# First layer of the block compression on two scaled 16-bit halves, in an NSA + forgetting-attention layer

## The chip, the cores and the metric

The kernel runs on one core of a Trainium2 chip. The metric is device time in microseconds (us) of one execution, the median of several runs. The core has five engines that run beside each other, each in its own program order: TensorE (PE; loading of its weights is shown apart as PEld), VectorE (DVE), ScalarE (ACT), GpSimd (POOL) and SyncE (SP), which here issues nearly all DMAs. Products land in PSUM, the rest lives in SBUF.

## The reference

One inference step of a decoder layer over 1024 prompt tokens and 8 x 8 sample tokens (512 cached tokens each), model width 1024, all in single precision. One projection gives the inputs of two head groups: native sparse attention with three branches (compressed blocks, selected blocks, window) and forgetting attention. The part that the change touches is the compression of the first branch's keys and values:

```python
def compress(x, pe, w1, w2):                      # CMP_LEN 32, CMP_STRIDE 16, hidden 128
    n_cmp = (L - CMP_LEN) // CMP_STRIDE + 1
    idx = np.arange(n_cmp)[:, None] * CMP_STRIDE + np.arange(CMP_LEN)[None, :]
    blocks = x[:, idx] + pe[None, None, :, None, :]
    h = jax.nn.silu(jnp.einsum('bnlgd,ldh->bngh', blocks, w1))
    return jnp.einsum('bngh,hd->bngd', h, w2)
...
kcmp = rms_norm(compress(kc, pe_k, w1k, w2k), gk_cmp)
vcmp = compress(vc, pe_v, w1v, w2v)
```

It is done once for the prompt and once for each of the 8 sample sequences over their cached pages; k and v have weights of their own.

## The kernel before

**Stages.** The first third projects the tokens: `w_in` is cut into 15 chunks of 256 to 288 columns, and for each chunk nine token tiles (eight of the prompt, one of the samples) are multiplied (`project`, L245 and L238). Tokens and projection weights stand as two half-precision halves, high and low, and each product is made of three (high by high, high by low, low by high). The chunks 0 to 10 go first; the rest is strewn into the forgetting attention of the prompt, followed by the sample attention strewn into the sparse attention, and the output projection.

**Compression.** It is a list of background functions, called at the fourth tile of a chunk: `cmp_weights` and `cmp_prompt_tokens` in chunk 1, `cmp_cached(0..3)` (two sequences each) in chunks 2 to 5, `sample_compressed` in chunk 6. `cmp_pairs` (L455) loads pairs of tokens (`cpair`, four buffers), transposes them on TensorE into the PSUM tile `ctr`, of which there is one buffer (L466), and copies them from there to `cx` (prompt) or `cy` (cache) on ScalarE (L468). `cmp_acc` (L474) multiplies: for each of k and v 16 products of 128 rows into the PSUM tile `sa`, of which there is one buffer too. In single precision, with 133 columns for the prompt (its blocks and the position embedding) and 128 for a cached group. `cmp_hidden` adds the bias and applies SiLU, and a second, small product (L508, L537) follows.

**Weights of the chunks.** `load_w` loads a chunk's weights in four parts into `wst` (four buffers), squares them on ScalarE with a running sum (`vsq`, L201), adds the sums up with a product by all-ones weights (L204), takes a power on GpSimd (L207), and splits the scaled weights into halves `wsp` (L215 to L220).

**What sets the order.** The functions above are written in program order, but the compiler's scheduler, with a timeline of its own, decides the order of each engine's queue; it moves background work between the products of a chunk. Tiles with the same tag share buffers, and a buffer is written again only when its last readers are done.

Of the kernel before, what the change touches and what calls it, by code (L numbers as in the profile page):

```python
# [11 lines left out]
F32 = mybir.dt.float32  # L12
F32R = mybir.dt.float32r
F16 = mybir.dt.float16
# [79 lines left out]
def layer_kernel(ctx, tc, a, o):  # L94
# [329 lines left out]
    cbias = C.tile([128, 2, 2], F32, name="cbias")  # L424
    cw = []

    def cmp_weights():
        cw.append(C.tile([128, 2, 16, 128], F32, name="cw", tag="vb16"))
        for kv in range(2):
            w1, w2 = ((a["w_cmp1_k"], a["w_cmp2_k"]), (a["w_cmp1_v"], a["w_cmp2_v"]))[kv]  # L430
            w1v = w1[0].rearrange("(s p) d h -> (p d) s h", p=2)
            for q in range(2):
                nc.sync.dma_start(cw[0][:, kv, 8 * q:8 * q + 8], w1v[:, 8 * q:8 * q + 8])
            nc.sync.dma_start(cw2[:, kv], w2[0])
        nc.vector.tensor_scalar(cw2, cw2, 0.5, None, op0=ALU.mult)

    def cmp_hidden(acc, kv, n, dst):
        t = C.tile([128, 130], F32, name="hth", bufs=1)
        u = C.tile([128, 130], F32, name="hb", bufs=1)
        nc.vector.tensor_scalar(u[:, :n], acc, cbias[:, kv, 0:1], None, op0=ALU.add)  # L440
        nc.scalar.activation(t[:, :n], acc, AF.Tanh, scale=0.5, bias=cbias[:, kv, 1:2])
        nc.vector.scalar_tensor_tensor(dst, t[:, :n], 1.0, u[:, :n], op0=ALU.add, op1=ALU.mult)
# [12 lines left out]
    def cmp_pairs(loads, dst):  # L455

        st = []
        for load in loads:
            x = C.tile([128, 4, 2, 64], F32, name="cpair", bufs=4)
            load(x)  # L460
            st.append(x)
        for kv in range(2):
            p = PS.tile([128, 2, 2, 128], F32, name="ctr", bufs=1)
            for j in range(2):
                for g in range(2):
                    nc.tensor.transpose(p[:, j, g], st[j][:, 2 * kv + g].rearrange("m p d -> m (p d)"), ident)  # L466
            for g in range(2):
                nc.scalar.activation(dst(kv, g), p[:, :, g].rearrange("p j (c r) -> p r j c", r=8), AF.Copy)  # L468

    def cmp_acc(kv, n, view):  # L470
        acc = PS.tile([128, 256], F32, name="sa", bufs=1)
        for i in range(16):
            h, r = divmod(i, 8)
            nc.tensor.matmul(acc[:, 0:n], cw[0][:, kv, i], view(h, r), start=(i == 0), stop=(i == 15))  # L474
        return acc

    def cmp_prompt_tokens():
        cx = [C.tile([128, 8, 134], F32, name=f"cx{kv}", tag=f"cy{kv}") for kv in range(2)]
        pet = C.tile([32, 128], F32, name="cpe", tag="grow")
        for kv in range(2):  # L480
            nc.gpsimd.memset(cx[kv][:, :, 64:66], 0.0)
            nc.gpsimd.memset(cx[kv][:, :, 130:132], 0.0)
            nc.sync.dma_start(pet[16 * kv:16 * kv + 16], (a["pe_cmp_k"], a["pe_cmp_v"])[kv][0].rearrange("(s p) d -> s (p d)", p=2))
        p = PS.tile([128, 2, 2, 128], F32, name="ctr", bufs=1)
        nc.tensor.transpose(p[:, 0, 0, 0:32], pet, ident[0:32, 0:32])
        for kv in range(2):
            nc.scalar.activation(cx[kv][:, :, 132:134],
                                 p[:, 0, 0, 16 * kv:16 * kv + 16].rearrange("p (h r) -> p r h", h=2), AF.Copy)

        def load(k):  # L490
            def f(x):
                for p in range(2):
                    nc.sync.dma_start(x[:, :, p], cmp_prompt[k, :, p])
            return f

        for q in range(2):
            cmp_pairs([load(2 * q), load(2 * q + 1)],
                      lambda kv, g: cx[kv][:, :, g * 66 + 32 * q:g * 66 + 32 * q + 32].rearrange("p r (j c) -> p r j c", j=2))
        for kv in range(2):
            acc = cmp_acc(kv, 133, lambda h, r: cx[kv][:, r, h:h + 133])  # L500
            nc.scalar.activation(cbias[:, kv, 0:1], acc[:, 132:133], AF.Copy)
            nc.scalar.activation(cbias[:, kv, 1:2], acc[:, 132:133], AF.Copy, scale=0.5)
# [11 lines left out]
    def cmp_cached(q):  # L514
        cy = [C.tile([128, 8, 4, 34], F32, name=f"cy{kv}", tag=f"cy{kv}") for kv in range(2)]
        for y in cy:
            nc.gpsimd.memset(y[:, :, :, 32:34], 0.0)
        for b in range(2):
            def load(k):
                def f(x):  # L520
                    for j in range(2):
                        src = cmp_pages[ds(page(2 * q + b, 2 * k + j), 1)]
                        for p in range(2):
                            nc.sync.dma_start(x[64 * j:64 * j + 64, :, p], src[:, :, p].rearrange("o m z d -> (o m) z d"))
                return f
            cmp_pairs([load(0), load(1)],
                      lambda kv, g: cy[kv][:, :, 2 * g + b, 0:32].rearrange("p r (j c) -> p r j c", j=2))
        for kv in range(2):
            acc = cmp_acc(kv, 128, lambda h, r: cy[kv][:, r, :, h:h + 32])
# [1083 lines left out]
```

## Time and profile before

| what | us |
|---|---|
| median of 3 runs | 976.82 |
| lowest and highest | 975.48, 977.11 |
| the profiled execution | 974.53 |
| its span | 972.8 |
| TensorE busy | 901.1 |
| VectorE, ScalarE, GpSimd busy | 644.9, 612.3, 397.4 |

The span goes from the first to the last instruction in the profile; the execution's own time has a little around it. Engines overlap, so their busy times don't add up to the span. A line number such as L474 is that of the kernel above. In a row of the timeline stand the start, the length of the merged piece, engine, line, operation, output and inputs, shapes and the count; idle time ahead of it and what ended it stand in brackets. A single-precision product leaves two records. Pieces of TensorE overlap, since products are pipelined, so pace is read from start to start.

### The profile page before, as it was taken

Reading aid. Unit: us, or ns where it says so; the run is one execution under the profiler, and the core shown is the slowest. Engines: PE = TensorE matmul, PEld = TensorE weight load, DVE = VectorE, ACT = ScalarE, POOL = GpSimd, SP = SyncE. Lnnn points to the kernel's source line nnn. Section 1 sums busy time; section 2 is a strip of 40 time slices with the busy share of each in tenths; the row PEclk is TensorE's granted clock in tenths of the full one; section 3 lists DMA queues with packets and bytes.
Section 4 is the critical chain, followed back from the end, with each engine's and each line's share of the span. In section 5 each row is a group of like instructions: output and inputs, shape, how many; then the busy total and the mean of one; then the engine's idle time right before and its main releaser. Section 6 shows DMA issues by size and latency. Waiting matters only on the chain.

```text
span 972.8 us, 24636 instructions
## 1 busy us (share of the span) xinstructions
PE 901.1 (93%) x9097; PEld 707.1 (73%) x9097; DVE 644.9 (66%) x1845; ACT 612.3 (63%) x1328; POOL 397.4 (41%) x571
## 2 busy tenths in 40 slices
PE   4898999889999999999998888889999979999997
PEld 3687889878888988878786556656666645776776
DVE  5764666564555426768777566887888989776552
ACT  6844643433454665797786779888897868454540
POOL 4544567754676432342425123434333157211100
PEclk9999999999999999999999899999999999999999
DMA  7563323422343332331314755555355032231241
GB/s 267 142 154 110 90 81 89 107 59 70 98 117 99 117 106 65 106 110 54 88 43 125 234 154 154 164 170 177 114 167 185 5 129 97 97 108 57 76 140 66
DMA packets 119740, 111.73 MB, mean 115 GB/s; under 512 B 37100, under 2 KB 100244, under 8 KB 119596
## 3 DMA queue, kind: packets, MB, share of 16 engines
q1 hardware_dynamic: 117732, 106.74, 36.4%
q0 software_dynamic: 1456, 2.83, 1.3%
q8 instruction: 71, 1.16, 0.5%
q10 hardware_dynamic: 432, 0.59, 0.2%
q14 instruction: 49, 0.40, 0.1%
HBM read 79.57 MB, written 27.41 MB: 110 GB/s over the span
## 4 chain that ended last, share of the span: by engine, by line
PE 64%; DVE 9%; DMA 7%; ACT 6%; issue 3%; POOL 2%; SPq 1%; DVEq 0%; ACTq 0%; POOLq 0%
PE acc L245 22%; PE ctr L1499 7%; PE sa L474 3%; PE acc L238 3%; PE smax L1054 2%; PE pv L726 2%; PE pv L724 2%; PE pv L725 2%; PE st L1098 2%; PE st L1099 2%; DMA wst<-in_w_in_dram 2%; DVE junk L744 2%; PE ctr L1547 1%; PE st L774 1%; PE st L775 1%
## 5 line engine op out<-in xcount | busy, mean ns | idle before, releaser
L245 PE MATMUL acc<-wsp,xth 128*128 128x256 f16 (+1 forms) x1920 | 334.7, 275 | 5.1 <-ACT xth L175 2.6
L245 PE MATMUL acc<-wsp,xtl 128*128 128x256 f16 (+1 forms) x960 | 264.1, 275 | 0.0
L245 PEld LDWEIGHTS <-xth 128*128 128x128 f16 x1920 | 187.3, 99 | 33.7 <-ACT xth L175 3.1
L1103 ACT ACTIVATE pf<-st,nsc 128x512 f32<-128x512 f32 x132 | 99.0, 780 | 49.6 <-PE st L1099 26.9
L245 PEld LDWEIGHTS <-xtl 128*128 128x128 f16 x960 | 94.5, 98 | 14.8 <-issue 1.4
L724 PEld LDWEIGHTS <-phi 128*128 128x128 f16 x816 | 76.9, 97 | 17.0 <-issue 5.5
L726 PEld LDWEIGHTS <-plo 128*128 128x128 f16 x816 | 76.7, 99 | 9.8 <-DVE plo L1106 2.4
L1104 ACT ACTIVATE phi<-pf 128x1024 f16<-128x1024 f32 (+1 forms) x76 | 71.7, 948 | 14.0 <-PE pv L726 8.8
L725 PEld LDWEIGHTS <-phi 128*128 128x128 f16 x816 | 76.8, 97 | 4.7 <-issue 1.5
L1106 DVE TENSOR_TENSOR plo<-pf,phi 128x1024 f16<-128x1024 f32 (+1 forms) x58 | 67.0, 1158 | 10.8 <-ACT phi L1104 10.0
L711 ACT ACTIVATE pf<-st,nsc 128x512 f32<-128x512 f32 (+1 forms) x96 | 62.5, 670 | 16.1 <-PE st L775 5.2
L264 POOL TENSOR_TENSOR nss<-nss,nhalf 128x4 f32<-128x4 f32 (+3 forms) x72 | 68.4, 950 | 4.4
L724 PE MATMUL pv<-va,phi 128*128 128x65 f16 x528 | 59.0, 193 | 4.3 <-DVE nt L1083 3.4
L716 DVE TENSOR_TENSOR plo<-pf,phi 128x512 f16<-128x512 f32 (+3 forms) x77 | 51.6, 674 | 16.0 <-ACT phi L714 15.7
L201 ACT ACTIVATE vsq<-wst 128x512 f16<-128x512 f32 (+2 forms) x72 | 40.2, 559 | 33.4 <-DMA wst<-in_w_in_dram 32.5
L725 PE MATMUL pv<-va,phi 128*128 128x64 f16 x528 | 58.9, 195 | 0.0
L726 PE MATMUL pv<-va,plo 128*128 128x65 f16 x528 | 56.4, 192 | 0.4 <-DVE plo L1106 0.2
L1106 POOL TENSOR_TENSOR plo<-pf,phi 128x1024 f16<-128x1024 f32 (+1 forms) x18 | 34.6, 1923 | 51.4 <-ACT phi L1104 40.6
L714 ACT ACTIVATE phi<-pf 128x512 f16<-128x512 f32 (+1 forms) x96 | 48.7, 524 | 10.3 <-PE pv L726 8.8
L1054 PE MATMUL smax<-kma,nqm 88*128 88x512 f16 (+3 forms) x192 | 49.1, 316 | 3.8 <-DVE nm L744 3.5
L1084 POOL TENSOR_TENSOR oa<-oa,nt 128x256 f32<-128x256 f32 x22 | 19.7, 894 | 78.8 <-DVE nt L1083 65.0
L1098 PE MATMUL st<-nqm,kma 88*128 88x512 f16 x132 | 50.2, 380 | 0.9 <-ACT pf L1103 0.7
(446 smaller groups left out, 2402.6 us busy)
## 6 DMA issues: line engine op xcount, KB each, us to landing
wst<-in_w_in_dram SPq DMA_DIRECT2D x56, 256.0 KB
sfk<-in_cache_fox_kv_dram SPq DMA_DIRECT2D x32, 256.0 KB
sfv<-in_cache_fox_kv_dram SPq DMA_DIRECT2D x32, 256.0 KB
out_dram<-kv SPq DMA_DIRECT2D x52, 128.0 KB
xin<-in_x_prompt_dram SPq DMA_DIRECT2D x8, 512.0 KB
cpair<-in_cache_nsa_cmp_kv_dram SPq DMA_DIRECT2D x64, 64.0 KB
zpark<-z SPq DMA_DIRECT2D x32, 128.0 KB
spg<-in_cache_nsa_slc_kv_dram SPq DMA_DIRECT2D x32, 128.0 KB
```

Source lines behind the costliest of these rows:

```text
L245: nc.tensor.matmul(ps[:, :n], x[:, k, t * 128:(t + 1) * 128], w[k // 2][:, i, k % 2, :n], start=(k == 0 and j == 0), stop=(k == KT - 1 and ...
L264: nc.gpsimd.tensor_tensor(ss[:n, 0, :h], ss[:n, 1, :h], nhalf[:n, :h], op=ALU.pow)
L711: nc.scalar.activation(p[:n, :cols], ps[:n, :cols], AF.Exp, bias=nsc[:n, 3:4], scale=nsc[:n, 6:7])
L724: nc.tensor.matmul(po[:, s, 0:65], hi[:, c], v[:, 0:65], start=f, stop=False, skip_group_check=True)
L725: nc.tensor.matmul(po[:, s, 0:64], hi[:, c], v[:, 65:129], start=False, stop=False, skip_group_check=True)
L726: nc.tensor.matmul(po[:, s, 0:65], lo[:, c], v[:, 0:65], start=False, stop=l, skip_group_check=True)
L1054: nc.tensor.matmul(pr[:, r], qm[0:88, (r0 + r) * 128:(r0 + r + 1) * 128], kma[0:88, 2 * k + g, j0 * 128:j1 * 128], start=r == 0, stop=not ...
L1098: nc.tensor.matmul(ps, kma[0:88, 2 * k + g, c], qm[0:88], start=True, stop=False)
L1103: nc.scalar.activation(pf[:, 512 * x:512 * x + 512], ps, AF.Exp, bias=nsc[:, 3:4], scale=nsc[:, 2:3])
L1104: nc.scalar.activation(hi[:, 0:n], pf[:, 0:n], AF.Copy)
L1106: (nc.gpsimd if turn[0] % share[mixed[0]] == 0 else nc.vector).tensor_sub(lo_[:, 0:n], pf[:, 0:n], hi[:, 0:n])
L1499: nc.tensor.matmul(ps, l[:, k], w[:, k, c], start=(k == 0 and j == 0), stop=(k == KT - 1 and j == 2))
```

## The change

The first layer's weights and tokens are held as two half-precision halves instead of in single precision. Weights (one scale each for k and v) and each group of tokens (likewise) are scaled by a power of their sum of squares, and the scales are taken out again in the bias and the activation. Each of the 16 single-precision products becomes three half-precision products.

```diff
+    def cmp_sums(sq, n):
+        p = PS.tile([128, 16], F32, name="sa", bufs=1)
+        nc.tensor.matmul(p[:, 0:2 * n], ones, sq.rearrange("p k n -> p (k n)"), start=True, stop=True)
+        s = C.tile([128, 2, 2], F32, name="cssum")
+        nc.vector.tensor_reduce(out=s[:, 0], in_=p[:, 0:2 * n].rearrange("p (k n) -> p k n", k=2), axis=AX.X, op=ALU.add)
+        nc.vector.tensor_scalar(s[:, 1], s[:, 0], 2.0 ** -30, TINY, op0=ALU.mult, op1=ALU.add)
+        return s
+
     def cmp_weights():
-        cw.append(C.tile([128, 2, 16, 128], F32, name="cw", tag="vb16"))
+        cw.append(C.tile([128, 2, 16, 2, 128], F16, name="cw", tag="vb16"))
...
-                nc.sync.dma_start(cw[0][:, kv, 8 * q:8 * q + 8], w1v[:, 8 * q:8 * q + 8])
+                r = B.tile([128, 8, 128], F32, name="xin", bufs=5)
+                nc.sync.dma_start(r, w1v[:, 8 * q:8 * q + 8])
+                junk = B.tile([128, 8, 128], F32, name="xsq")
+                nc.scalar.activation(junk, r, AF.Square, accum_out=sq[:, kv, q:q + 1])
+                raw.append(r)
...
+        s = cmp_sums(sq, 2)
+        nc.gpsimd.tensor_tensor(cws[:, :, 0], s[:, 1], nhalf[:, 0:2], op=ALU.pow)
+        for kv in range(2):
+            for q in range(2):
+                hi, lo = (cw[0][:, kv, 8 * q:8 * q + 8, z] for z in (0, 1))
+                nc.scalar.activation(hi, raw[2 * kv + q], AF.Copy, scale=cws[:, kv, 0:1])
+                nc.vector.scalar_tensor_tensor(lo, raw[2 * kv + q], cws[:, kv, 0:1], hi, op0=ALU.mult, op1=ALU.subtract)
...
+    def cmp_scales(sq, n):
+        s = cmp_sums(sq, n)
+        nc.gpsimd.tensor_tensor(cws[:, :, 1], s[:, 1], nhalf[:, 0:2], op=ALU.pow)
+        nc.vector.tensor_tensor(s[:, 0], cws[:, :, 0], cws[:, :, 1], op=ALU.mult)
+        nc.vector.reciprocal(cws[:, :, 2], s[:, 0])
+        nc.vector.tensor_scalar(cws[:, :, 3], cws[:, :, 2], 0.5, None, op0=ALU.mult)
...
-    def cmp_pairs(loads, dst):
+    def cmp_load(loads, sq):
...
+            for kv in range(2):
+                junk = C.tile([128, 2, 2, 64], F32, name="cjunk", bufs=1)
+                nc.scalar.activation(junk, x[:, 2 * kv:2 * kv + 2], AF.Square, accum_out=sq[:, kv, i:i + 1])
...
+    def cmp_halves(kv, p, hi, lo):
+        nc.scalar.activation(hi, p, AF.Copy, scale=cws[:, kv, 1:2])
+        nc.vector.scalar_tensor_tensor(lo, p, cws[:, kv, 1:2], hi, op0=ALU.mult, op1=ALU.subtract)
...
             for g in range(2):
-                nc.scalar.activation(dst(kv, g), p[:, :, g].rearrange("p j (c r) -> p r j c", r=8), AF.Copy)
+                cmp_halves(kv, p[:, g].rearrange("p j m -> p (j m)").rearrange("p (c r) -> p r c", r=8), *dst(kv, g))
...
-            nc.tensor.matmul(acc[:, 0:n], cw[0][:, kv, i], view(h, r), start=(i == 0), stop=(i == 15))
+            for j, (w, x) in enumerate(((0, 0), (0, 1), (1, 0))):
+                nc.tensor.matmul(acc[:, 0:n], cw[0][:, kv, i, w], view(x, h, r), start=(i == 0 and j == 0),
+                                 stop=(i == 15 and j == 2))
```

In `cmp_prompt_tokens` and `cmp_cached` all four pairs are now loaded and squared by `cmp_load`, `cmp_scales` follows, and then come the transposes, two pairs at a time as before. The prompt's position embedding is squared too and shares the prompt's scale.

The scheduler's order changes with it. On TensorE, around the first products of the compression (the prompt's keys), the order before reads as follows; `cx` are the prompt's tokens, `acc` the projection:

```order
L245 MATMUL acc<-wsp,xtl 128x256
L466 MATMUL ctr<-ident,cpair 128x128 x4
L474 MATMUL sa<-cx_992,cw 128x133 x16
L245 LDWEIGHTS xth
L245 MATMUL acc<-wsp,xth 128x256
```

and in the changed kernel, where L508 are the transposes and L517 the products:

```order
L517 LDWEIGHTS cw
L517 MATMUL sa<-cx_1020,cw 128x133
L245 LDWEIGHTS xth
L245 MATMUL acc<-wsp,xth 128x288
L245 LDWEIGHTS xtl
L245 MATMUL acc<-wsp,xtl 128x288
L245 LDWEIGHTS xth
L245 MATMUL acc<-wsp,xth 128x288
L245 LDWEIGHTS xth
L245 MATMUL acc<-wsp,xth 128x288
L508 MATMUL ctr<-ident,cpair 128x128 x4
L517 LDWEIGHTS cw
```

The first product now stands in the next chunk (288 columns), and the last transposes stand between the first product and the other 47.

On ScalarE, the copies out of `ctr` of the second cached group (`cy`) stand before among squares of chunk weights (L201) and of projections (L261):

```order
L261 ACTIVATE nsq<-acc 128x256
L201 ACTIVATE vsq,vst<-wst 128x2x256
L468 ACTIVATE cy_2197<-ctr 128x8x32 x2
L201 ACTIVATE vsq,vst<-wst 128x2x256
L261 ACTIVATE nsq<-acc 128x256
L201 ACTIVATE vsq,vst<-wst 128x2x256 x2
L468 ACTIVATE cy_2198<-ctr 128x8x32 x2
```

and in the changed kernel, with the copies at L499 and the squares of the next group's token pairs at L494:

```order
L499 ACTIVATE cy_2428<-ctr,cws 128x8x32
L261 ACTIVATE nsq<-acc 128x256
L494 ACTIVATE cjunk,csq_3130<-cpair 128x256 x2
L261 ACTIVATE nsq<-acc 128x256
L499 ACTIVATE cy_2427<-ctr,cws 128x8x32
L494 ACTIVATE cjunk,csq_3130<-cpair 128x256 x2
L201 ACTIVATE vsq,vst<-wst 128x2x256
L499 ACTIVATE cy_2427<-ctr,cws 128x8x32
L201 ACTIVATE vsq,vst<-wst 128x2x256
L261 ACTIVATE nsq<-acc 128x256
L201 ACTIVATE vsq,vst<-wst 128x2x256 x2
```

The two copies of a buffer, adjacent before, are apart, and squares that wait for page loads stand between them, beside those that wait for weights.

On VectorE, late in the program at the last head of the forgetting attention, the order before is (`plo` is the low half of probabilities, `l` and `obt` end a head, `sms` are statistics of a sample's softmax):

```order
L716 TENSOR_TENSOR plo<-pf,phi 128x384
L716 TENSOR_TENSOR plo<-pf,phi 128x128
L782 RECIPROCAL l<-pv 128x4
L783 TENSOR_SCALAR l<-l,vsc 128x4
L786 TENSOR_TENSOR obt<-pv,l 128x4x64
L1227 TENSOR_REDUCE sms<-ctr 128x1
L1228 TENSOR_REDUCE sms<-ctr 128x1
```

and in the changed kernel (L716 has become L771, L782 to L786 are L837 to L841, L1227 is L1282):

```order
L771 TENSOR_TENSOR plo<-pf,phi 128x384
L791 TENSOR_TENSOR nqm<-smax,block 24x512
L771 TENSOR_TENSOR plo<-pf,phi 128x128
L1282 TENSOR_REDUCE sms<-ctr 128x1
L1283 TENSOR_REDUCE sms<-ctr 128x1
L837 RECIPROCAL l<-pv 128x4
L1284 TENSOR_SCALAR sms<-sms 128x1
L838 TENSOR_SCALAR l<-l,vsc 128x4
L841 TENSOR_TENSOR obt<-pv,l 128x4x64
```

No line of that part was edited; the sample's softmax has moved ahead of the end of the head. Between about chunk 9 and this place the order is the same in both, but for single rows.

More of the change, by code (lines that the diff above doesn't have):

```diff
@@ L453, in cmp_norm, with cmp_pairs @@
                                            op0=ALU.mult, op1=ALU.mult)
-    def cmp_pairs(loads, dst):
+    def cmp_load(loads, sq):
         st = []
-        for load in loads:
+        for i, load in enumerate(loads):
             x = C.tile([128, 4, 2, 64], F32, name="cpair", bufs=4)
             load(x)
+            for kv in range(2):
+                junk = C.tile([128, 2, 2, 64], F32, name="cjunk", bufs=1)
+                nc.scalar.activation(junk, x[:, 2 * kv:2 * kv + 2], AF.Square, accum_out=sq[:, kv, i:i + 1])
             st.append(x)
+        return st
+    def cmp_halves(kv, p, hi, lo):
+        nc.scalar.activation(hi, p, AF.Copy, scale=cws[:, kv, 1:2])
+        nc.vector.scalar_tensor_tensor(lo, p, cws[:, kv, 1:2], hi, op0=ALU.mult, op1=ALU.subtract)
+    def cmp_pairs(st, dst):
         for kv in range(2):
@@ L494, in load @@
             return f
+        st = cmp_load([load(k) for k in range(4)], sq)
+        cmp_scales(sq, 5)
+        p = PS.tile([128, 2, 2, 128], F32, name="ctr", bufs=1)
+        nc.tensor.transpose(p[:, 0, 0, 0:32], pet, ident[0:32, 0:32])
+        for kv in range(2):
+            cmp_halves(kv, p[:, 0, 0, 16 * kv:16 * kv + 16].rearrange("p (h r) -> p r h", h=2),
+                       *(cx[kv][:, z, :, 132:134] for z in range(2)))
         for q in range(2):
-            cmp_pairs([load(2 * q), load(2 * q + 1)],
-                      lambda kv, g: cx[kv][:, :, g * 66 + 32 * q:g * 66 + 32 * q + 32].rearrange("p r (j c) -> p r j c", j=2))
+            cmp_pairs(st[2 * q:2 * q + 2],
+                      lambda kv, g: [cx[kv][:, z, :, g * 66 + 32 * q:g * 66 + 32 * q + 32]
+                                     for z in range(2)])
         for kv in range(2):
-            acc = cmp_acc(kv, 133, lambda h, r: cx[kv][:, r, h:h + 133])
-            nc.scalar.activation(cbias[:, kv, 0:1], acc[:, 132:133], AF.Copy)
-            nc.scalar.activation(cbias[:, kv, 1:2], acc[:, 132:133], AF.Copy, scale=0.5)
+            acc = cmp_acc(kv, 133, lambda x, h, r: cx[kv][:, x, r, h:h + 133])
+            nc.scalar.activation(cbias[:, kv, 0:1], acc[:, 132:133], AF.Copy, scale=cws[:, kv, 2:3])
+            nc.scalar.activation(cbias[:, kv, 1:2], acc[:, 132:133], AF.Copy, scale=cws[:, kv, 3:4])
             hs = C.tile([128, 130], F32, name="chs", tag="qsp", bufs=1)
@@ L514, in cmp_cached, with load, f @@
     def cmp_cached(q):
-        cy = [C.tile([128, 8, 4, 34], F32, name=f"cy{kv}", tag=f"cy{kv}") for kv in range(2)]
+        cy = [C.tile([128, 2, 8, 4, 34], F16, name=f"cy{kv}", tag=f"cy{kv}") for kv in range(2)]
+        sq = C.tile([128, 2, 4], F32, name="csq4")
         for y in cy:
-            nc.gpsimd.memset(y[:, :, :, 32:34], 0.0)
-        for b in range(2):
[L519 to L527, printed above, removed]
+            nc.gpsimd.memset(y[:, :, :, :, 32:34], 0.0)
+        def load(b, k):
+            def f(x):
+                for j in range(2):
+                    src = cmp_pages[ds(page(2 * q + b, 2 * k + j), 1)]
+                    for p in range(2):
+                        nc.sync.dma_start(x[64 * j:64 * j + 64, :, p], src[:, :, p].rearrange("o m z d -> (o m) z d"))
+            return f
+        st = cmp_load([load(b, k) for b in range(2) for k in range(2)], sq)
+        cmp_scales(sq, 4)
+        for b in range(2):
+            cmp_pairs(st[2 * b:2 * b + 2],
+                      lambda kv, g: [cy[kv][:, z, :, 2 * g + b, 0:32] for z in range(2)])
         for kv in range(2):
-            acc = cmp_acc(kv, 128, lambda h, r: cy[kv][:, r, :, h:h + 32])
+            acc = cmp_acc(kv, 128, lambda x, h, r: cy[kv][:, x, r, :, h:h + 32])
             hs = C.tile([128, 130], F32, name="chs", tag="qsp", bufs=1)
```

23 lines of the change are left out of this document (13 added, 10 removed).

## The prediction

> **What bounds the kernel now.** I read the engine totals and the chain that ended last first, then the busy time by stretch, then the waits of TensorE (PE) in the stretch that the change touches, then the rows of the instructions themselves.
>
> ```profile
> PE 901.1 (93%) x9097; PEld 707.1 (73%) x9097; DVE 644.9 (66%) x1845; ACT 612.3 (63%) x1328; POOL 397.4 (41%) x571
> ...
> PE 64%; DVE 9%; DMA 7%; ACT 6%; issue 3%; POOL 2%; SPq 1%; DVEq 0%; ACTq 0%; POOLq 0%
> PE acc L245 22%; PE ctr L1499 7%; PE sa L474 3%; PE acc L238 3%; PE smax L1054 2%; PE pv L726 2%; PE pv L724 2%; PE pv L725 2%; PE st L1098 2%; PE st L1099 2%; DMA wst<-in_w_in_dram 2%; DVE junk L744 2%; PE ctr L1547 1%; PE st L774 1%; PE st L775 1%
> ```
>
> TensorE is busy for 93% of the span and holds 64% of the chain. The products that the change rewrites (L474) are 3% of the chain, some 29 us, so they are worth having on the path. The next table has the stretch, its length, then busy us and instructions of PE, weight load, DVE, ACT and POOL, then the clock and the DMA.
>
> ```profile
> 50.00:80.00 30.00, 27.35 (x248) 24.33 (x246) 18.15 (x79) 14.58 (x43) 12.80 (x24) 1.00 0.67 177
> 80.00:250.00 170.00, 162.20 (x1459) 144.14 (x1458) 99.29 (x353) 72.73 (x214) 102.04 (x176) 1.00 0.31 81
> ```
>
> The compression runs from about 50 to 250 us, strewn between the projection products of chunks 1 to 5. In the main stretch PE is busy 162 of 170 us at full granted clock, while ACT, DVE and POOL have 97, 71 and 68 us free. The waits of PE from 45 to 300 us are these three (total, times, longest):
>
> ```profile
> PE ctr L466 <- ACT cy L468: 6.0, 4, 2.6
> PE ctr L466 <- ACT cx L468: 2.6, 1, 2.6
> PE ctr L537 <- DVE lw L607: 1.8, 1, 1.8
> ```
>
> PE waits 8.6 us for the one PSUM buffer `ctr` that the transposes of token pairs share, and hardly for anything else. So a microsecond taken from PE here is nearly a microsecond of the kernel, unless the new work on ACT and DVE makes those waits longer. One of them, in rows:
>
> ```profile
> 112.00 0.63 ACT L201 ACTIVATE vsq<-wst 128x512 f16<-128x512 f32 x1 [1.41 <-DMA wst<-in_w_in_dram]
> ...
> 113.90 0.66 ACT L468 ACTIVATE cy<-ctr 128x256 f32<-128x256 f32 x2
> ...
> 114.62 0.55 PE L466 MATMUL ctr<-ident,cpair 128*128 128x128 f32 x3 [0.75 <-ACT cy L468]
> ```
>
> ACT works in order; a square of the next chunk's weights waits for its DMA, the copy that empties `ctr` stands behind it, and PE waits for the copy. The copies themselves take 0.66 us.
>
> **The change part by part: the products.** One set of products (one of k or v, one group of blocks) is 16 single-precision products before and 48 half-precision ones after. There are ten sets: two of 133 columns for the prompt and eight of 128 for the cache.
>
> ```profile
> 118.73 3.74 PE L474 MATMUL sa<-cy,cw 128*128 128x128 f32 x32
> 122.31 0.28 PE L245 MATMUL acc<-wsp,xth 128*128 128x288 f16 x1
> ...
> 77.07 3.81 PE L474 MATMUL sa<-cx,cw 128*128 128x133 f32 x32
> 80.72 0.38 PE L245 MATMUL acc<-wsp,xth 128*128 128x256 f16 x2
> ...
> 703.77 0.20 PE L726 MATMUL pv<-va,plo 128*128 128x65 f16 x1
> ...
> 704.14 0.19 PE L726 MATMUL pv<-va,plo 128*128 128x65 f16 x1
> 704.17 0.61 PE L1027 MATMUL smax<-ident,nqs 128*128 128x128 f16 x8
> 704.61 0.38 PE L1098 MATMUL st<-nqm,kma 88*128 88x512 f16 x1
> ```
>
> From its own start to the start of what follows, a set takes 122.31 - 118.73 = 3.58 us at 128 columns (32 records, two for each product) and 80.72 - 77.07 = 3.65 us at 133. The nearest half-precision row is eight products of 128 columns, each with weights of its own, in 704.61 - 704.17 = 0.44 us: 55 ns each. That the weight load isn't the limit there shows in the products of 65 columns above them, which also load 128x128 weights each time: 12 steps in 704.14 - 703.77 = 0.37 us, 31 ns each. So 48 products take 48 x 55 ns = 2.64 us, and 2.74 us at 133 columns. The gain is 0.94 us for each of eight sets and 0.91 for each of two: 7.5 + 1.8 = **9.3 us off PE**.
>
> A rule speaks against this. The Trainium skill, "TensorE: Matmul & The Clock Gate", section "Back-to-back issue gap", gives some 81 ns for each product of 128 columns in a sustained stream of weight loads and products. By it a set would take 48 x 81 = 3.89 us, more than now, and the ten sets would cost some 3 us. The trace of this kernel doesn't agree: 55 ns with a load each, 31 ns at 65 columns.
>
> **Small products.** Six sums (one of the weights, five of tokens) go through PE as a product of a few single-precision columns with all-ones weights. The kernel has that already:
>
> ```profile
> 135.74 0.27 PE L245 MATMUL acc<-wsp,xtl 128*128 128x256 f16 x1
> 135.85 0.28 PE L204 MATMUL tr<-vst,ones 128*128 128x4 f32 x2
> 136.00 0.38 PE L245 MATMUL acc<-wsp,xth 128*128 128x256 f16 x2
> ```
>
> It takes the place of 136.00 - 135.85 = 0.15 us, so six add **0.9 us**. Transposes and second-layer products stay as they are. PE in sum: -9.3 + 0.9 = -8.4 us.
>
> **ACT and DVE.** The new work, with its nearest rows:
>
> ```profile
> L201 ACT ACTIVATION_READ_ACCUMULATOR vsq<-wst 128x1 f32 x20 | 3.8, 189 | 0.0
> L261 ACT ACTIVATE nsq<-acc 128x256 f32<-128x256 f32 x27 | 10.2, 378 | 18.2 <-PE acc L245 18.2
> L468 ACT ACTIVATE cy<-ctr 128x256 f32<-128x256 f32 x32 | 10.4, 380 | 8.4 <-PE ctr L466 8.4
> L219 ACT ACTIVATE wsp<-wst,vst 128x512 f16<-128x512 f32 x10 | 7.2, 716 | 8.3 <-POOL vst L207 8.3
> L307 DVE SCALAR_TENSOR_TENSOR vb<-acc,un,vb 128x256 f16<-128x256 f32 x16 | 7.8, 485 | 21.9 <-ACT vb L306 20.7 <-PE acc L238 1.2
> L220 DVE SCALAR_TENSOR_TENSOR wsp<-wst,vst,wsp 128x512 f16<-128x512 f32 x16 | 15.0, 937 | 6.2 <-ACT wsp L219 5.9 <-DMA slp<-in_cache_fox_logf_dram 0.2
> L206 DVE TENSOR_SCALAR vst<-vst 128x1 f32<-128x1 f32 x10 | 1.5, 149 | 0.1
> ...
> L207 POOL TENSOR_TENSOR vst<-vst,nhalf 128x1 f32<-128x1 f32 x6 | 3.5, 582 | 0.4
> ```
>
> ACT squares 40 halves of token pairs with a running sum: 40 x (0.378 + 0.189) = 22.7 us. The four weight quarters of 1024 columns are squared and scaled to 16 bits; I take two 512-column rows for each pass: 4 x 2 x (2 x 0.716) = 11.5 us at most. The 40 copies out of `ctr` stay, at 0.38 us each. DVE gets 40 remainders of 256 columns out of PSUM, 40 x 0.485 = 19.4 us, four of the weights at up to 2 x 0.937, 7.5 us, and some 27 operations on two columns, 27 x 0.149 = 4.0 us. POOL gets six small powers, 6 x 0.582 = 3.5 us. In the long stretch that would put ACT at (72.7 + 34) / 170 = 63% and DVE at about (99.3 + 31) / 170 = 77%, even with all of it inside. No engine passes PE, so I cost this work at nothing; what hides it is the 162 us of projection and compression products. If that cover were gone, it is ACT's 34 us that would show.
>
> **The release of `ctr`.** Before, the buffer comes free 0.66 us after the transposes. After, it takes copy, remainder, remainder: 0.38 + 2 x 0.485 = 1.35 us, and waits in two queues. But the order of PE has moved too: between two groups of transposes of one cached set stood 26 to 36 projection products, now 41 to 60. One product is the 48th part of this:
>
> ```profile
> 136.14 5.26 PE acc L245 x48
> ```
>
> That is 110 ns, so the distance grows from 2.9-4.0 us to 4.5-6.6 us. Less the release, 2.2-3.3 us were left for queues before, 3.1-5.2 us are left now. I take the 8.6 us of waits as unchanged: nothing gained and nothing lost, with zero and about three times their size as ends.
>
> **Loads.** The same four weight DMAs now land in the token buffers `xin`, earlier. In SP's order the first stands right behind the last token tile, and two stand ahead of chunk 2's weights, which PE needs only a chunk later. All four pairs must be there before the first transpose, and ACT's squares stand in line for them. DMA bytes don't change. I cost both at nothing; a late pair stalls ACT, as under the rival below.
>
> **The later half.** The scheduler's order changes again from the last attention heads on, where nothing was edited. There PE waits for many things a little:
>
> ```profile
> 600.00:700.00 100.00, 91.05 (x1117) 62.88 (x1114) 83.95 (x268) 81.78 (x165) 39.69 (x54) 0.98 0.52 161
> 700.00:760.00 60.00, 57.02 (x778) 39.37 (x778) 47.00 (x124) 53.04 (x107) 19.08 (x26) 1.00 0.49 150
> ```
>
> PE is idle 12 of 160 us. A new order may save or add a third of that, so 4 us either way; I take zero.
>
> **Sum.** The profiled execution took 974.53 us, 1.7 us more than its span; less 8.4 us that is 966.1. The median before is 976.82, 2.3 us above the profiled one, so against the median I forecast **968.4 us**, with 964 to 974 as its own range from the later half and small shifts in the waits.
>
> **Rivals.**
>
> *The transposes wait longer (slower).* Place: `ctr`, between two groups of transposes. DVE is a second queue in the release, and these are the longest waits of each:
>
> ```profile
> DVE nx L279 <- POOL nss L264: 28.5, 27, 3.4
> ACT vsq L201 <- DMA wst<-in_w_in_dram: 21.2, 15, 4.2
> ```
>
> It decides once the queues together hold more than the 3.1 us left; 4.2 + 3.4 would. The five waits before average 1.7 us. If 15 of the 20 groups waited that long, it would be 25.8 us in place of 8.6: 976.8 - 8.4 + 17.2 = 985.6 us. Against it stands that most of those DVE waits are near 1 us (28.5 / 27). Chance 0.18.
>
> *The gain is lost elsewhere (no change).* The pace is then set by the weight loading (ACT waits 21 us for it) or the later order takes 6 to 10 us back. Time 975 to 979. Against it: PE never waits for `wsp` in that stretch. Chance 0.14.
>
> *The waits vanish (faster still).* With more products between the transposes all 8.6 us may go: 976.8 - 8.4 - 8.6 = 959.8 us. Against it: their cause, a late DMA in ACT's line, is untouched. Chance 0.12.
>
> *Weight loads show (the products aren't faster).* If a half-precision load of 98 ns were laid bare at each product:
>
> ```profile
> L245 PEld LDWEIGHTS <-xtl 128*128 128x128 f16 x960 | 94.5, 98 | 14.8 <-issue 1.4
> ```
>
> a set takes 48 x 98 = 4.70 us, ten sets cost 11.2 more than now, with the sums 12.1: 988.9 us. The 31 ns above speak against it. Chance 0.04. The Trainium skill's 81 ns, from the page named above, would give 3.1 + 0.9, some 981 us.
>
> **How the numbers follow.** Forecast 0.52, waits vanish 0.12: faster 0.64. No change 0.14. The two slower rivals 0.18 + 0.04 = 0.22. A measurement of this kernel tells about 0.2% (2 us) from no change; the bounds are 974.9 and 978.8. The range runs from 960, the waits vanishing, to 981, which takes in half of the slower rival with fewer groups waiting; about 2 in 10 is left out.
>
> **What would show it.** Right: sets of 48 products from start to next start in 2.65 us; sums at 0.15 us each; PE waits at the transposes at or below 8.6 us; the first load of cached pages for sampling and all later work some 8 us earlier. Wrong: spacing of 80 ns or more; waits of the transposes, now named after DVE's remainder, above 17 us; ACT idle before the squares for the page DMA with PE idle behind it; or the gain present at 300 us and gone at the end, which would be the later order.

## The result, and the profile after

The changed kernel took **988.95 us** (median of 4 runs, 984.73 to 995.12) against 976.9 us before: ratio 1.0127, 95% interval 1.0089 to 1.0165. It is slower by some 12 us, where 968.4 us (960 to 981) had been forecast. Run again later beside the kernel before it took 988.85 us (ratio 1.0131 [1.0111, 1.0152]). The profiled execution took 995.12 us, the longest of the four; its span is 993.2 us. Ratios and their intervals, here and below, leave out one execution of e1 (1044.66 us at a granted clock of 0.842, where all others have 0.97 or more), and they are not always the quotient of the medians beside them. Busy totals and the chain that ended last, from the page after:

```profile
PE 905.5 (91%) x9269; PEld 705.6 (71%) x9269; DVE 671.9 (68%) x1919; ACT 646.0 (65%) x1424; POOL 402.1 (40%) x577
...
PE 49%; DVE 11%; DMA 8%; POOL 7%; ACT 6%; issue 4%; SPq 1%; DVEq 0%; ACTq 0%; POOLq 0%
```

TensorE's share of the chain fell from 64% to 49%; POOL, 2% before, has 7%. ACT grew by 34 us and DVE by 27, about what the prediction had counted. So the amounts came true and the gain did not: TensorE itself is busy for 905.5 us, 4.4 more than before, and more of the chain lies on other engines.

To find where, I cut the span at two places that both kernels have: the start of the first projection product of chunk 1, and that of chunk 11. What stands ahead of the first mark varies between executions (60.0 us in one profile of the changed kernel, 57.1 in the next), so stages are counted from there. First the kernel before, then the changed one; start and end of the stretch, its length, busy us and instructions of PE, weight load, DVE, ACT, POOL, then PE's clock and the DMA:

```profile
57.90:364.40 306.50, 294.54 (x2676) 260.47 (x2674) 162.93 (x592) 145.07 (x396) 179.16 (x289) 1.00 0.35 98
364.40:972.80 608.40, 566.54 (x6134) 413.68 (x6133) 442.01 (x1143) 425.70 (x819) 191.88 (x230) 0.98 0.38 115
```

```profile
60.00:371.50 311.50, 294.74 (x2856) 256.73 (x2855) 189.89 (x666) 174.04 (x485) 185.50 (x295) 0.98 0.33 93
371.50:993.20 621.70, 572.71 (x6134) 418.34 (x6133) 442.45 (x1143) 428.34 (x819) 190.21 (x230) 0.97 0.38 113
```

Two things show. Chunks 1 to 10, where the gain was to be, take 5.0 us more. And the rest, in which no line was edited and TensorE has the same number of records, 6134, takes 13.3 us more: it is busy for 6.2 us more on them and idle for 7.1 us more.

**In the first stretch** the products did get shorter. The timeline of PE after, at the prompt's keys (start, length, engine, line):

```profile
111.05 2.95 PE L517 MATMUL sa<-cx,cw 128*128 128x133 f16 x47
113.83 0.29 PE L245 MATMUL acc<-wsp,xtl 128*128 128x288 f16 x1
```

47 products of 133 columns take 113.83 - 111.05 = 2.78 us, 59 ns each; of 128 columns they take 2.70 us (from 191.09 us on), 57 ns each. But PE waits for other things now (waits from 45 to 300 us; total, times, longest):

```profile
PE tr L204 <- ACT vsq L201: 4.1, 1, 4.1
PE sa L517 <- ACT cy L499: 3.1, 2, 2.2
PE ctr L508 <- issue: 2.5, 2, 2.3
PE ctr L543 <- DMA cpe<-in_pe_cmp_v_dram: 1.6, 1, 1.6
PE tr L170 <- DVE xtl L176: 1.6, 1, 1.6
PE ctr L508 <- DVE cy L500: 1.3, 2, 1.1
```

A wait for `issue` is one for which the profile shows no reason. The transposes, which were the place of the slower rival, wait less than before (2.5 + 1.3 us against 8.6). The longest wait stands in the projection itself. These are the rows of ACT and of PE around it:

```profile
77.01 4.27 ACT L456 ACTIVATE cw<-xin,cws 128x1024 f16<-128x1024 f32 x4 [0.97 <-POOL cws L452]
...
83.54 0.63 ACT L201 ACTIVATE vsq<-wst 128x512 f16<-128x512 f32 x1
84.07 0.19 ACT L201 ACTIVATION_READ_ACCUMULATOR vsq<-wst 128x1 f32 x1
```

```profile
79.89 0.27 PE L245 MATMUL acc<-wsp,xtl 128*128 128x256 f16 x1
84.31 0.39 PE L204 MATMUL tr<-vst,ones 128*128 128x4 f32 x2 [4.15 <-ACT vsq L201]
85.83 0.58 PE L245 MATMUL acc<-wsp,xth 128*128 128x256 f16 x2 [1.14 <-DVE va L307]
```

ACT copies the compression's weights for 4.27 us; the squares of the next chunk's weights stand behind that, their sum (L204) stands in PE's queue ahead of projection products, and PE is idle for 4.15 + 1.14 us. The squares of the compression's own token pairs stand in ACT's line too, and ahead of them it is idle for 21.2 us (count, busy us, mean ns of one, then the idle time and what ended it):

```profile
L494 ACT ACTIVATE cjunk<-cpair 128x256 f32<-128x256 f32 x40 | 16.6, 415 | 21.2 <-DMA cpair<-in_cache_nsa_cmp_kv_dram 19.0 <-DMA cpair<-out_dram 1.8
```

The granted clock halves behind the wait at L204, and once more later (windows after; the clock is the figure before the last two):

```profile
84.60:91.40 6.80, 5.67 (x28) 4.14 (x29) 4.61 (x23) 3.17 (x9) 5.67 (x13) 0.50 0.15 49
149.50:152.90 3.40, 3.40 (x34) 3.40 (x33) 3.05 (x10) 2.11 (x7) 3.03 (x6) 0.50 0.88 254
```

In these 10.2 us PE is busy for 5.67 + 3.40 = 9.07 us, so half clock cost up to 4.5 us, an estimate. Before, the same stretch ran at full clock throughout. That is the largest part of why PE's busy time did not fall although its products did.

### The profile page after: what moved, and what is told of

Its sections match the earlier page's. It is cut to its first block, busy times and chain, and to the rows that moved or that the text cites. A ratio compares the mean times of both kernels' runs of the same rounds, so it can differ in the third digit from the quotient of the medians.

```text
span 993.2 us, 25195 instructions
## 1 busy us (share of the span) xinstructions
PE 905.5 (91%) x9269; PEld 705.6 (71%) x9269; DVE 671.9 (68%) x1919; ACT 646.0 (65%) x1424; POOL 402.1 (40%) x577
## 4 chain that ended last, share of the span: by engine, by line
PE 49%; DVE 11%; DMA 8%; POOL 7%; ACT 6%; issue 4%; SPq 1%; DVEq 0%; ACTq 0%; POOLq 0%
PE acc L245 13%; PE ctr L1554 7%; POOL nss L264 2%; PE pv L781 2%; PE pv L780 2%; PE pv L779 2%; PE st L1153 2%; PE smax L1109 2%; PE st L1154 2%; DVE plo L1161 1%; DMA nq<-qpark 1%; PE acc L238 1%; PE st L829 1%; PE st L830 1%; PE ctr L1602 1%
## 5 line engine op out<-in xcount | busy, mean ns | idle before, releaser
L779 PEld LDWEIGHTS <-phi 128*128 128x128 f16 x816 | 78.0, 98 | 16.4 <-issue 3.6
L780 PEld LDWEIGHTS <-phi 128*128 128x128 f16 x816 | 77.9, 99 | 3.3 <-issue 0.5
L771 DVE TENSOR_TENSOR plo<-pf,phi 128x512 f16<-128x512 f32 (+3 forms) x77 | 51.9, 680 | 15.0 <-ACT phi L769 13.7
L1153 PE MATMUL st<-nqm,kma 88*128 88x512 f16 x132 | 50.8, 385 | 6.9 <-ACT pf L1158 6.7
L769 ACT ACTIVATE phi<-pf 128x512 f16<-128x512 f32 (+1 forms) x96 | 49.2, 528 | 10.1 <-PE pv L781 7.8
L201 ACT ACTIVATE vsq<-wst 128x512 f16<-128x512 f32 (+2 forms) x72 | 40.3, 564 | 23.7 <-DMA wst<-in_w_in_dram 23.2
L799 DVE CUSTOM_DVE_ANT_0 junk<-smax,maskw,nm 128x512 bf16<-128x512 f32 x64 | 47.7, 745 | 6.9 <-PE smax L1109 5.0
```

Of the source, the lines that this page charges most:

```text
L779: nc.tensor.matmul(po[:, s, 0:65], hi[:, c], v[:, 0:65], start=f, stop=False, skip_group_check=True)
L780: nc.tensor.matmul(po[:, s, 0:64], hi[:, c], v[:, 65:129], start=False, stop=False, skip_group_check=True)
L1153: nc.tensor.matmul(ps, kma[0:88, 2 * k + g, c], qm[0:88], start=True, stop=False)
```

## The experiments

Four questions: does the later order cost what it seems to; what in the first stretch eats the gain; is a microsecond of PE there worth one; and can the loss be avoided. Each result stands against runs of the kernel before on the same chip (974.66 us for e1 to e4, 975.64 for e5 to e8, 976.31 for e9 to e11); a difference between kernels of two of these groups is uncertain by as much as these medians differ. No kernel computes less than the reference unless it is said.

**e1: the changed kernel with the old order after chunk 11.** In all kernels here the late part has one of two orders on TensorE, apart from some 90 rows at most; small shifts of the scheduler's timeline decide which. Four idle writes, which end up at the program's start, turn it back:

```diff
     fox_operands(C2, ("km1", "qm1", "k11", "q11"))
+    nc.vector.memset(PJ.tile([128, 512], BF16, name="junk", bufs=1), 0.0)
+    nc.vector.memset(PJ.tile([128, 512], BF16, name="junk", bufs=1), 0.0)
+    nc.vector.memset(PJ.tile([128, 512], BF16, name="junk", bufs=1), 0.0)
+    nc.vector.memset(PJ.tile([128, 512], BF16, name="junk", bufs=1), 0.0)
```

> The changed kernel with four small idle VectorE memsets at the program's start. They leave its order in the first stage as it is, but the scheduler then gives the last attention heads, the sample stage and the output projection the order of the kernel before. Theory A (both matter: the first stage loses time by stalls, and the new late order loses more): the forgetting attention starts near 371 us as in the changed kernel (before: 363), and the rest runs as before, so the whole takes 980 to 984 us. Rival B (only the late order is bad): 968 to 976 us. Rival C (only the first stage and the clock are bad, the order is nothing): 987 to 991 us, as the changed kernel.

Measured 981.15 us, ratio 1.0048 [1.002, 1.0076]: theory A's range. Against the changed kernel's 988.85 that is 7.7 us for order alone. In the traces the 6134 records of PE after chunk 11 stand in e1 in the very order of the kernel before, and take 609.9 us against its 608.4.

**e2: the kernel before with the new order.** The same four writes in the kernel before give it nearly the changed kernel's late order: in the traces 61 of PE's 6134 records stand otherwise.

> The kernel before with the same four idle memsets, by which the late stages get the order of the changed kernel nearly row by row, while its first stage stays as it was. Theory A: the forgetting attention starts near 364 us, the rest is 5 to 9 us longer than before: 982 to 986 us. Rival B (only the late order is bad): 987 to 991 us. Rival C (the order is nothing): 975 to 979 us.

Measured 988.53 us, ratio 1.0119 [1.0069, 1.017]. An old kernel with old products, slowed as much as by the change. It is more than theory A expected and in theory B's range; its profile has 616.1 us after chunk 11 against 608.4 before, 7.7 us more, and chunk 11 starts 4.0 us later, 2.7 of them lost ahead of chunk 1. So the 7.7 us are the order's; why the rest is lost is not shown, and whether the idle writes take time themselves was not tried apart. That order is nothing (theory C) is refuted from both sides.

What the new order does shows in the late part of e1, cut at the transposes ahead of the output projection, and of the changed kernel's second profile (e8, below):

```profile
371.50:781.30 409.80, 380.50 (x4551) 280.73 (x4551) 307.23 (x871) 326.33 (x679) 141.78 (x190) 0.98 0.42 125
781.30:981.40 200.10, 186.94 (x1585) 134.32 (x1584) 133.92 (x273) 98.98 (x141) 50.34 (x40) 0.99 0.28 94
```

```profile
367.70:779.80 412.10, 375.50 (x4444) 278.38 (x4443) 296.49 (x849) 319.90 (x667) 139.23 (x187) 0.97 0.42 125
779.80:989.00 209.20, 195.33 (x1692) 139.24 (x1690) 146.22 (x295) 108.50 (x153) 51.03 (x43) 0.99 0.28 90
```

The orders agree up to 549 us of the changed kernel's first profile (542 in the kernel before); all of the loss lies behind that. 107 PE instructions, 8.4 us of work, moved behind the second mark, and 9.1 us more are spent there. Ahead of it PE has 5.0 us less to do, and yet that stretch takes 2.3 us longer: its idle time went from 29.3 to 36.6 us. Of the 11.4 us in all, 8.0 are idle time and 3.4 a longer busy time of PE on the same records, with 30.7 us at half clock after chunk 11 against 21.8. The waits of PE there, first e1, then e8:

```profile
PE smax L790 <- DVE mh L788: 7.0, 4, 4.9
PE ctr L1376 <- ACT sfkt L1377: 3.6, 2, 2.7
PE pv L779 <- DVE nt L1142: 3.4, 2, 2.0
...
PE st L1157 <- ACT pf L1162: 0.9, 3, 0.4
```

```profile
PE st L1153 <- ACT pf L1158: 7.1, 6, 2.5
PE smax L790 <- DVE mh L788: 6.2, 3, 4.9
PE ctr L1297 <- ACT spr L1287: 3.9, 3, 2.6
PE ctr L1352 <- ACT son L1350: 3.3, 4, 1.6
```

The scores of the sparse attention (`st`, L1153 or L1157) wait for the exponentials (`pf`) that free their PSUM: 7.1 us, 0.9 with the old order. The sample's own waits (`spr`, `son`) come on top. That less is at hand for PE just when ACT is late, since the sample's work is interleaved otherwise, is a reading of these rows; no run tries it.

**e3 and e4: constant scales.** In e3 all scales are constants (2048 for weights, 16 for tokens), so there are no squares, sums and powers; loads, halves and 48 products stay. In e4 only the weights' scale is constant. Such constants suit these inputs; they don't follow the data.

```diff
+    for i, v in enumerate((2048.0, 16.0, 1.0 / 32768, 0.5 / 32768)):
+        nc.vector.memset(cws[:, :, i], v)
...
-                nc.scalar.activation(junk, r, AF.Square, accum_out=sq[:, kv, q:q + 1])
...
-                nc.scalar.activation(junk, x[:, 2 * kv:2 * kv + 2], AF.Square, accum_out=sq[:, kv, i:i + 1])
...
-        cmp_scales(sq, 5)
...
-        cmp_scales(sq, 4)
```

> The changed kernel with constant scales: no squares of weights and tokens, no sums, no powers. Halves, remainders on VectorE and the 48 half-precision products stay; the late stages have the order of the kernel before. It leaves the computation of the scales out. Theory A, squares and scales as the cause in the first stage (ScalarE's line and the wait for all four pairs): the forgetting attention starts 6 to 9 us earlier than before, near 355 to 358 us, and the whole takes 967 to 971 us. Rival D (the remainders on VectorE and the release of ctr are the cause): it starts near 368 to 371 us and the whole takes 980 to 984 us.

> The changed kernel with a constant scale for the weights alone: their squares, their sum and the wait for it are left out, the tokens are still squared and scaled. The late order is nearly that of the kernel before. Theory A1 (the weights' work in ScalarE's line is what costs in the first stage: it held up the square of chunk 3's weights for 4.1 us and let the granted clock fall to half): the forgetting attention starts near 361 to 365 us, the whole takes 973 to 978 us. Theory A2 (the tokens' squares and their wait for page loads are what costs): it starts near 367 to 371 us, the whole takes 979 to 984 us.

e3 took 975.81 us, ratio 1.0012 [0.9985, 1.0039]; e4 984.71, ratio 1.0099 [1.007, 1.0127]. e3 missed both ranges and lies between: the squares matter, and without them the change still doesn't gain its 8 us in the total. e4 is where its second theory put it (979 to 984), if anything above: the weights' squares are nearly harmless, those of the tokens are not. The wait at L204, the longest in the changed kernel, is gone in e4, and chunk 1 to 11 still takes 309.4 us, 1.2 less than in e8; so that wait alone is not what eats the gain. Both have the old late order (609.9 and 608.8 us after chunk 11), so their difference of 9 us lies ahead of it: 7.9 us in chunks 1 to 10 (301.5 and 309.4 in the profiles) and 2.9 ahead of chunk 1. In chunks 1 to 10 e3 has gained:

```profile
61.40:362.90 301.50, 289.71 (x2844) 254.11 (x2843) 177.03 (x630) 152.12 (x399) 179.56 (x289) 0.99 0.34 96
```

301.5 us against 306.5, 5.0 of them, and 4.8 less of busy PE.

**e5: the squares alone.** The old kernel, to which the loading of four pairs at once, the 40 squares of the tokens, the sums and powers are added; their results are not used.

```diff
+            for kv in range(2):
+                junk = C.tile([128, 2, 2, 64], F32, name="cjunk", bufs=1)
+                nc.scalar.activation(junk, x[:, 2 * kv:2 * kv + 2], AF.Square, accum_out=sq[:, kv, i:i + 1])
...
+        cmp_scales(sq, 4)
```

> The old kernel with its single-precision products and plain copies, and beside them the new kernel's loading of four pairs at once, the squares of the tokens, their sums and powers, whose results nothing uses. The order from chunk 11 on is the old one but for some 30 rows. Theory A2 (the tokens' squares in ScalarE's line, with their waits for the loads, delay the projection's own work): the first stage takes 9 to 11 us more as between e3 and e4, chunk 11 starts at 372 to 375 us, the time is 982 to 986. Rival D (squares cost only because the copies need the scale that comes out of them): chunk 11 starts at 364 to 367, the time is 974 to 978.

Measured 985.4 us, ratio 1.0105 [1.0087, 1.0124]; chunk 1 to 11 took 315.5 us, 9.0 more than before:

```profile
59.40:374.90 315.50, 300.97 (x2686) 264.94 (x2684) 167.36 (x615) 160.39 (x467) 184.10 (x294) 0.98 0.34 94
```

Theory A2. Of PE's work only the sums read these squares, and none of PE's waits in that stretch is at a sum; so it isn't the longer chain to the copies that costs. This is their group on ACT in e5: count, busy us and mean ns of one, then ACT's idle time ahead of them and what ended it:

```profile
L483 ACT ACTIVATE cjunk<-cpair 128x256 f32<-128x256 f32 x40 | 16.6, 415 | 31.9 <-DMA cpair<-in_cache_nsa_cmp_kv_dram 26.4 <-DMA cpair<-out_dram 5.2
L483 ACT ACTIVATION_READ_ACCUMULATOR cjunk<-cpair 128x1 f32 x40 | 7.7, 192 | 0.0
```

24.3 us of work, as predicted (22.7), and 31.9 us in which ACT stands in front of a square whose load has not landed, up to 4.1 us at a time, with everything behind it.

**e9: the same squares without the wait for loads.** To tell standing still from working, the 40 squares of e5 read the copies that come out of the transposes instead of the loaded pairs: same size, same number, same number of sums, which now stand behind the transposes. The loading of four pairs at once stays. Against e5:

```diff
-                nc.scalar.activation(junk, x[:, 2 * kv:2 * kv + 2], AF.Square, accum_out=sq[:, kv, i:i + 1])
...
                 nc.scalar.activation(dst(kv, g), p[:, :, g].rearrange("p j (c r) -> p r j c", r=8), AF.Copy)
+                junk = C.tile([128, 8, 2, 16], F32, name="cjunk", bufs=1)
+                nc.scalar.activation(junk, dst(kv, g), AF.Square, accum_out=sq[:, kv, g:g + 1])
```

> As e5 (old products, squares and sums that nothing uses), but the 40 squares of the cached and prompt tokens read the copies that come out of the transposes in place of the pairs that the loads bring. They have the same size and number, and no longer wait for a load ahead of other work. From chunk 11 on the old order but for four rows. Theory W (e5's loss is ScalarE standing still for loads with the projection's own work behind it): chunk 1 to chunk 11 takes 306 to 310 us against 306.5 before and 315.5 in e5, the time is 975 to 979. Rival Q (it is the squares' own 23 us on ScalarE, and the sums): 313 to 317 us, the time is 983 to 987.

Measured 977.99 us, ratio 1.003 [1.0002, 1.0059]; chunk 1 to 11 took 309.8 us. Theory W. The stretch, and the larger of the two groups on ACT:

```profile
58.50:368.30 309.80, 299.67 (x2686) 265.70 (x2684) 164.75 (x615) 161.39 (x467) 182.56 (x294) 0.98 0.35 97
...
L494 ACT ACTIVATE cjunk<-cy 128x256 f32<-128x256 f32 x32 | 13.6, 424 | 0.4
```

The same work, next to no idle time ahead of it, and 7.4 us less in the total. So of the 9 to 10 us that the squares cost, some two thirds (5.7 of 9.0 us in the stretch) to four fifths (8.1 of 9.8 us, each total against its own kernel before) go with ACT's standing in front of loads, and the work itself is nearly hidden, as the prediction had it. The clock doesn't make this difference: both have 10.2 us at half clock in the stretch, where the kernel before has none, and of the 5.7 us between them 4.4 are idle time of PE (14.5 and 10.1 us).

**e6 and e10: what a microsecond of PE is worth.** e6 is e3 with only the product of the high halves, 320 products fewer; the low halves are made and not used. In e10 the low halves of the tokens aren't made either (with three idle writes for the old late order). Both leave out two of the three products, so they compute less exactly and are no candidates.

```diff
-            for j, (w, x) in enumerate(((0, 0), (0, 1), (1, 0))):
+            for j, (w, x) in enumerate(((0, 0),)):
...
```

> As e3 (constant scales), but of the three products only high by high is made: 320 products fewer on TensorE, 320 x 55 ns = 17.6 us; halves are still made, so ScalarE and VectorE have the same work. The product is less exact. Theory P (TensorE sets the pace of the first stage, as the prediction said): 14 to 18 us of it show, chunk 11 starts at 345 to 349, the time is 958 to 962. Rival R (the chain copy, remainder, product, activation through the single buffers, and the loads, set the pace of the compression): at most half of it shows, chunk 11 starts at 354 or later, the time is 967 or more.

> As e6 (constant scales, high by high only), and the low halves of the tokens are not made either: 40 remainders fewer on VectorE. Three idle writes at the program's start give the old order from chunk 11 on but for some 70 rows. Theory H (the remainders are hidden under TensorE): within 2 us of e6, 960 to 964. Rival R (the remainders cost what e3 lacks: it gained 5 us from chunk 1 to 11 where TensorE was to give 9): 955 to 959.

e6 took 961.78 us (ratio 0.9847 [0.9829, 0.9866]), 14.0 less than e3; chunk 1 to 11 took 286.4 us, 15.1 less:

```profile
63.60:350.00 286.40, 272.41 (x2524) 235.80 (x2523) 178.61 (x632) 150.92 (x400) 179.46 (x288) 0.99 0.36 101
```

320 products at 59 ns are 18.9 us, so three quarters to four fifths show: theory P by the time, though chunk 11 starts at 350.0, a little after its mark. e10 took 964.68 us (ratio 0.9901 [0.987, 0.9933]); its stretch is 285.9 us. That is 0.7 us above theory H's range and 2.9 above e6, so rival R, which asked for less time, is refuted: the 40 remainders on DVE cost nothing that shows.

**e7: constant scales, and the work moved.** e3 with the position embedding loaded ahead of the weights, and the weights' constant scale made from a value that arrives with chunk 2's weights, so that their split leaves chunk 0.

```diff
     def cmp_weights():
+        for kv in range(2):
+            nc.sync.dma_start(pet[16 * kv:16 * kv + 16], (a["pe_cmp_k"], a["pe_cmp_v"])[kv][0].rearrange("(s p) d -> s (p d)", p=2))
+        nc.vector.tensor_scalar(cws[:, :, 0], vsc[:, 1, 0:2], 0.0, 2048.0, op0=ALU.mult, op1=ALU.add)
...
```

> As e3 (constant scales), but the position embedding is loaded ahead of the weights, and the weights' constant scale is made from a value that comes with chunk 2's weights, so that the split of the weights leaves chunk 0. Order from chunk 11 on as of old. Theory S (place, not amount: e3 lost 3.5 us in chunk 0 because VectorE split weights there, and 2 us by the embedding's late load): chunk 1 starts at 57.5 to 59.5 us, chunk 11 at 358 to 360, the time is 970 to 973. Rival R (the amount of work on VectorE and ScalarE sets it, wherever it stands): chunk 1 starts earlier but chunk 11 at 362 to 364, the time is 974 to 977.

Measured 972.51 us, ratio 0.9973 [0.9951, 0.9995]: the only one with all the products that is faster than the kernel before. The total is that of theory S, its marks are not: chunk 1 starts at 60.6 us and chunk 11 at 362.9, as in e3, and the difference lies after chunk 11 (605.6 us). So it beats both kernels by a little, but why it beats e3 isn't shown.

**e8: the changed kernel again**, to see that its first profile was no odd one.

> The changed kernel itself, on the same chip as e5 to e7. Theory A: 986 to 991, chunk 11 starts at 371 to 372 us and some 620 us follow it, as in its first profile. If its first profile was an odd one, under 984.

988.85 us; chunk 11 starts at 367.7, earlier than expected and 3.8 us earlier than in the first profile, 2.9 of them won ahead of chunk 1. From chunk 1 to 11 it took 310.6 us, and 621.3 after: the same two losses. It waits 3.3 us at L204 and halves its clock for 6.8 and 3.4 us, as in the first profile.

**e11: the scales from squares, but later.** The changed kernel with the embedding loaded first and the compression one chunk later.

```diff
-    background = {1: [cmp_weights, cmp_prompt_tokens], 2: [lambda: cmp_cached(0)], 3: [lambda: cmp_cached(1)],
+    background = {2: [cmp_weights, cmp_prompt_tokens], 3: [lambda: cmp_cached(0)], 4: [lambda: cmp_cached(1)],
...
```

> The changed kernel with its scales from squares, but the position embedding is loaded ahead of the weights, and the compression starts one chunk later (weights and prompt in chunk 2, the cache in chunks 3 to 6). From chunk 11 on the old order but for some 75 rows. Theory S (place: loads have more time, ScalarE is not held up): 975 to 979. Rival Q (the squares cost the same wherever they stand): 981 to 985, as e1 and e4.

Measured 983.56 us, ratio 1.009 [1.0056, 1.0123]: rival Q by its number, but not by its reason. The squares' group in it:

```profile
L498 ACT ACTIVATE cjunk<-cpair 128x256 f32<-128x256 f32 x40 | 16.5, 412 | 26.2 <-DMA cpair<-in_cache_nsa_cmp_kv_dram 18.9 <-DMA cpair<-out_dram 3.6 <-issue 2.4
```

The stretch took 318.1 us in a profile that lies 6.7 us above the median. A chunk later the squares still meet loads that have not landed. The loads have four buffers, which the group before holds until its own transposes are done, so they may move with the rest; that this is the reason was not tried.

## Why the prediction was wrong

*The products: right, over-sized.* A set was to fall from 3.58 to 2.64 us at 55 ns a product, or to 2.74 at 133 columns, 57 ns; the products run at 57 and 59 ns. The groups of all ten sets, first before, then after, and the sums:

```profile
L474 PE MATMUL sa<-cy,cw 128*128 128x128 f32 x256 | 30.9, 276 | 0.0
...
L474 PE MATMUL sa<-cx,cw 128*128 128x133 f32 x64 | 7.9, 278 | 0.0
```

```profile
L517 PE MATMUL sa<-cy,cw 128*128 128x128 f16 x384 | 26.3, 229 | 4.2 <-ACT cy L499 3.1 <-ACT hth L472 1.0
...
L517 PE MATMUL sa<-cx,cw 128*128 128x133 f16 x96 | 6.3, 222 | 0.8 <-ACT cx L499 0.8
L431 PE MATMUL sa<-csq,ones 128*128 128x8 f32 (+1 forms) x10 | 1.8, 250 | 0.5 <-ACT hth L472 0.4
```

38.8 us became 32.6, a gain of 6.2 us in place of 9.3. From start to start, with idle time left out, it is 6.9 us, and half clock took 1.6 of what is missing: 47 products took 4.30 us from 149.43 us on, in place of 2.70. The six sums take 1.2 us from start to start, not 0.9. The rival of bare weight loads (98 ns) is refuted, and the trace doesn't follow the 81 ns of the Trainium skill's page "TensorE: Matmul & The Clock Gate", section "Back-to-back issue gap", either.

*That PE's time is the kernel's time there: right.* In e6 some four fifths of the time of the products left out show in the stretch.

*"No engine passes PE, so I cost this work at nothing": the first step that failed.* The amounts on ACT and DVE were right, and e9 and e10 show that the work as such is nearly hidden. But ACT takes its instructions in order, and each square that reads a pair stops it until the pair has landed: 21.2 us of idle time in the changed kernel, 31.9 in e5. The prediction had the rule in its hands ("a late pair stalls ACT, as under the rival below") and priced it only where the transposes wait. The waits at the transposes fell; which wait of PE each stop led to is not shown one by one, but the projection's squares and copies stand in the same line, and e9 shows that most of the loss goes when the stops go. Adding ACT's shares of busy time says nothing of that: ACT was busy for 47% of the stretch before (145.07 of 306.5 us) and is for 56% now. The squares cost 9.0 us of the stretch in e5 and 9.8 us of the total.

*"I take the 8.6 us of waits as unchanged": close in sum, wrong as an account.* The transposes of pairs, which the 8.6 us were about, wait 2.5 + 1.3 = 3.8 us now; with the waits at `sa` and at the embedding's transposes (3.1 + 1.6) it is 8.5 us, by luck. New is the wait at L204, 4.1 us, with a granted clock at half behind it, which the prediction had no term for.

*"A new order may save or add ... 4 us either way; I take zero": the second step that failed.* It costs 8 us by the medians of e1 and e8, 11 by what follows chunk 11 in their profiles. The bound of a third of PE's idle time in 160 us was too narrow: the order differs from 549 us on, over more than 400 us, and a longer busy time of PE counts as well. The prediction named the sign that tells of this ("the gain present at 300 us and gone at the end") but gave such a loss 6 to 10 us only as a way back to no change.

Together, by the first profile: from chunk 1 to 11 the changed kernel lost 5.0 us, 294.74 - 294.54 = 0.2 us of it more busy PE and 16.8 - 12.0 = 4.8 us more idle PE. The 0.2 us are, from start to start with idle time left out: the compression's products -6.9, the sums +1.2, the transposes of pairs +1.2 (eight of their records stood ahead of the first mark before), and +4.5 on the projection's own high- and low-half products of the prompt, 1920 as before, on which half clock fell; 0.2 are spread over the rest. After chunk 11 it lost 13.3 us, 6.2 of them more busy PE on the same 6134 records, with 38.1 us at half clock against 20.5, and 7.1 idle. With 2.1 us ahead of chunk 1 that is 20.4 us, more than the 12 us between the medians, as the first profile lies 6.2 us above the median of its kernel and that of the kernel before 2.4 us below. The rival that came nearest in time is the one of bare weight loads (988.9 us); that is luck, since its mechanism is refuted. The slower transposes (985.6) had the right cause, a late load in ACT's line, but put its cost at the transposes, which wait less.

## What to carry to other kernels

Work on an engine that is half idle was not free here, as its instruction waited for a DMA: count what stands behind it in that engine's queue, and price the wait, not the busy time. When a compiler's scheduler sets the order, a change in one stage can turn the order of another; compare the orders before reading a time, and where they differ, bring the changed kernel back to the old order by something idle, so that change and order are timed apart. A precision split that needs a scale from the data pays for that scale: here it cost more than the faster products brought.

## What the runs showed of the hardware

The granted clock of TensorE falls to half for 3.4 us, or a multiple of that, shortly after many of the gaps of 2 us or more from one start of a product to the next. In the changed kernel's first profile, from 60 us on, seven of nine such gaps are followed by it: after 4.4 us from 79.9 us on it is half from 84.6 to 91.4, and after 2.5 us from 145.9 on from 149.5 to 152.9. The length fits the window of about 3.4 us that the Trainium skill gives in "TensorE: Matmul & The Clock Gate", section "What's actually happening"; the second gap is shorter than the one idle window that it asks for. Not every such gap is followed by one: 2.9 us at 73.7 us in the kernel before was not. And two spells of the changed kernel, at 576.1 and 658.1 us, have no such gap shortly ahead of them. So the idle 4.15 us at L204 cost some 7 us, by an estimate that adds half of the 5.67 us that PE then worked at half clock.
